# Turning the gated unit's output by VectorE blocks and on-chip transfers instead of by TensorE

## The chip, the cores and the metric

The kernel runs on one core of a Trainium2 chip. The metric is the device time of one execution in microseconds (us). A profile of one execution shows what each engine did: PE is TensorE (PEld its weight loads), DVE is VectorE, ACT is ScalarE, POOL is GpSimd, SP is the engine that issues most transfers (SPq in rows). Each engine takes its instructions strictly in the order in which the program lists them.

## The reference, cut to what matters

Two layers, each with one mixer over 256 tokens of width 2048. All columns come from one input projection. The change touches the gated unit of the convolution branch: `u` is made token by token, and the convolution runs along the tokens, channel by channel.

```python
proj = jnp.einsum("bsd,de->bse", h, w_in[layer])
q, k, v, g_att, glu_a, glu_b, g_conv = jnp.split(proj, SPLIT_POINTS, axis=-1)
...
u = glu_a * jax.nn.sigmoid(glu_b)
u = jnp.pad(u, ((0, 0), (CONV_WIDTH - 1, 0), (0, 0)))
y = lax.conv_general_dilated(u, dw_kernel.astype(u.dtype)[:, None, :], window_strides=(1,),
                             padding="VALID", dimension_numbers=("NWC", "WIO", "NWC"),
                             feature_group_count=D_CONV) + dw_bias
y = jax.nn.silu(layer_norm(y, ln_g, ln_b))
return jnp.einsum("bsc,ce->bse", y, w_pw)
```

## The kernel before, in words

All matrix products are cut into groups of 512 output columns, 40 for each layer, and each group into 8 tiles: 640 tiles in one fixed order, numbered 0 to 639 here. A tile is 256 rows of weights, 512 KB. Four things happen to tile i. SP issues its load into one of four buffers `raw` (`load`, line 222). ACT copies it to the rounded half `whi` (line 229). DVE forms the rest `wlo` by a subtraction (line 230). PE runs 12 matmuls on it (lines 616 to 618), the second of which is the first to need `wlo`. The load of tile i stands on SP right behind the split of tile i-4, whose buffer it takes, and `whi` and `wlo` have four buffers each, so a split of tile i can start when PE has finished tile i-4.

All other work is written as generators, and a planner (`Filler`) with its own clock for each engine places their slices between the tiles when the program is built. So the order on every engine is fixed; a slice that comes late on the chip holds what is listed behind it.

For each block j of 512 channels (four in a layer) the groups are glu_b, glu_a, v, q, k. `ev_glu_b` leaves the sigmoid in `Dt[0]`, 128 partitions (tokens) by 2 token halves by 512 channels. `ev_glu_a` multiplies it in place by glu_a on DVE (line 314). Then PE turns the result by 8 transposes through the identity into two PSUM banks (`transposes`, line 256), and ACT copies the banks to `uT` (line 322), which has channels on partitions. The convolution (`conv`, lines 336 and 339) reads `uT` on DVE, 124 operations for each j. In the first layer and j = 1, which the rows below follow, glu_a is tiles 48 to 55 and the transposes stand on PE between tiles 56 and 57.

Of the kernel before, what the change touches and what calls it, by code (L numbers as in the profile page):

```python
# [13 lines left out]
AF = mybir.ActivationFunctionType  # L14
# [3 lines left out]
SEQ = 256  # L18
# [3 lines left out]
PAD = CW - 1  # L22
KT = D // 128
NCH = 4
CH = 512
# [14 lines left out]
class Need:  # L40
# [3 lines left out]
    def __init__(self, banks=0, when=None, **time):  # L44
        self.banks, self.when, self.time = banks, when, list(time.items())
# [5 lines left out]
class Filler:  # L51
# [7 lines left out]

    def __init__(self, banks, horizon, patience):  # L60
        self.tasks = []
        self.t = dict(P=0.0, V=0.0, A=0.0, G=0.0)
        self.horizon, self.patience = horizon, patience
        self.banks = [(b, 0.0) for b in banks]
        self.count = 0
# [80 lines left out]
def trunk(ctx: ExitStack, tc: tile.TileContext, x, w_in, q_norm_g, k_norm_g, w_pw, w_out, x_t, gains, params,  # L146
          rope_cos, rope_sin, log_count, out):
    nc = tc.nc
# [4 lines left out]
    V, S, G, T = nc.vector, nc.scalar, nc.gpsimd, nc.tensor  # L153

    def t(shape, name, dt=F32):
        return sb.tile(shape, dt, name=name)
# [5 lines left out]
    A = [t([128, 2, CH], f"a{c}") for c in range(4)]  # L162
# [3 lines left out]
    uT = [t([128, 4, PAD + SEQ], f"ut{i}") for i in range(2)]  # L166
# [3 lines left out]
    qT, kT = (C[i].rearrange("p (h s) -> p h s", h=4) for i in (1, 2))  # L170
    Dt = [t([128, 2, CH], f"d{i}") for i in range(3)]
    t2 = t([128, CH], "t2")
    sm = [t([128, 384], f"sm{i}") for i in range(4)]
    junk = t([128, CH], "junk", BF16)
    ident = t([128, 128], "ident")
# [21 lines left out]
    fill = Filler([pp.tile([128, CH], F32, name=f"ax{i}") for i in range(4)], dict(V=4.5, A=3.5), 5)  # L197
# [41 lines left out]
    def flag(*what):  # L239
        flags.add(what)  # L240

    def has(*what):
        return lambda: what in flags
# [6 lines left out]
    def transposes(src, banks):  # L250

        for b in range(2):
            for i in range(2):
                for tt in range(2):
                    e = (2 * b + i) * 128
                    T.transpose(banks[b][:, i * SEQ + tt * 128:i * SEQ + tt * 128 + 128],  # L256
                                src[:, tt, e:e + 128], ident)

    def to_stationary(src, s, c, gain):

        yield Need(2, lambda: vacant[s][c], P=0.9)
        banks = [fill.bank(), fill.bank()]
        transposes(src, banks)
        yield Need(A=1.5, V=1.6)
        p = [b[:, i * SEQ:(i + 1) * SEQ] for b in banks for i in range(2)]
        for i in range(4):
            S.activation(st_hi[s][c][:, i], p[i], AF.Copy, scale=gain(i))  # L267
        for i in range(4):
            V.scalar_tensor_tensor(st_lo[s][c][:, i], p[i], gain(i), st_hi[s][c][:, i].bitcast(F32),  # L269
                                   op0=ALU.mult, op1=ALU.subtract)  # L270
        fill.free(*banks)
        filled(s, c)

    def filled(s, c):
        vacant[s][c] = False
        ready[s][c] = True
# [12 lines left out]
    def x_chunk(l, c):  # L289

        yield from to_stationary(A[c], 0, c, lambda i: ng[:, l * KT + 4 * c + i:l * KT + 4 * c + i + 1])
        fill.add(x_square(l, c), 3, fill.now[4])
# [18 lines left out]
    def ev_glu_a(l, j, ps):  # L311
        yield Need(0, has("ev", l, "glu_b", j), V=1.4)
        for tt in range(2):
            V.scalar_tensor_tensor(Dt[0][:, tt], ps[tt], rx[:, tt:tt + 1], Dt[0][:, tt],
                                   op0=ALU.mult, op1=ALU.mult)
        flag("ev", l, "glu_a", j)
        yield Need(2, has("conv", l, j - 2) if j >= 2 else None, P=0.9)
        banks = [fill.bank(), fill.bank()]
        transposes(Dt[0], banks)
        yield Need(A=1.0)  # L320
        for b in range(2):
            S.activation(uT[j % 2][:, 2 * b:2 * b + 2, PAD:], banks[b].rearrange("p (c s) -> p c s", c=2), AF.Copy)
        fill.free(*banks)
        flag("glu", l, j)
        fill.add(conv(l, j), 5 + j, fill.now[4])

    def conv(l, j):
        u = uT[j % 2]
        y = Y[j].rearrange("p (c s) -> p c s", c=4)
        w = prm[:, 4 * j:4 * j + 4]  # L330
        for k in range(CW):
            for c in range(4):
                if c % 2 == 0:
                    yield Need(V=0.8)
                if k == 0:
                    V.tensor_scalar(y[:, c], u[:, c, 0:SEQ], w[:, c, l * CW:l * CW + 1], w[:, c, P_BIAS + l:P_BIAS + l + 1],
                                    op0=ALU.mult, op1=ALU.add)
                else:
                    V.scalar_tensor_tensor(y[:, c], u[:, c, k:k + SEQ], w[:, c, l * CW + k:l * CW + k + 1], y[:, c],  # L339
                                           op0=ALU.mult, op1=ALU.add)  # L340
        flag("conv", l, j)
        for c in range(4):
            yield Need(0, has("ysum", l, j - 1) if j else None, G=0.7)
            if j == 0 and c == 0:
                G.tensor_copy(ysum, y[:, c])
            else:
                G.tensor_add(ysum, ysum, y[:, c])  # L347
        flag("ysum", l, j)
        if j == NCH - 1:
            fill.add(layer_norm(l), 4, fill.now[4])  # L350
# [166 lines left out]
    def ev_g_att(l, j, ps):  # L517
        yield Need(0, has("attsq", l, j), A=1.2, V=1.2)
        for tt in range(2):
            S.activation(Dt[0][:, tt], ps[tt], AF.Silu, scale=rx[:, tt:tt + 1])  # L520
        V.tensor_mul(A[j], A[j], Dt[0])
        flag("ev", l, "g_att", j)
        yield from to_stationary(A[j], 0, j, lambda i: prm[:, 4 * j + i, P_ATT + l:P_ATT + l + 1])
        src = x[0, :, j * CH:(j + 1) * CH] if l == 0 else xs[j]
        nc.sync.dma_start(A[j], src.rearrange("(t p) e -> p t e", p=128))
# [7 lines left out]
    def ev_pw(l, j, ps):  # L533
        yield Need(A=1.2, V=1.2)
        y = Y[j].rearrange("p (t e) -> p t e", t=2)
        for tt in range(2):
            V.tensor_mul(y[:, tt], ps[tt], GC[j][:, tt])
            S.activation(junk, ps[tt], AF.Square, accum_out=ssf[:, tt, j:j + 1])
        flag("ev", l, "pw", j)
        if j == NCH - 1:  # L540
            yield Need(V=0.1, G=0.6)
            V.tensor_reduce(rsc, ssf, axis=mybir.AxisListType.X, op=ALU.add)
            rsqrt(rc, rsc, 1.0 / D, 2)
            flag("rc", l)
        yield from to_stationary(y, 1, j, lambda i: prm[:, 4 * j + i, P_CONV + l:P_CONV + l + 1])
# [44 lines left out]
    for c in range(NCH):  # L590
        fill.add(first_chunk(c), 0)
    split(0)


    users = {"glu_b": ev_glu_b, "glu_a": ev_glu_a, "v": ev_v, "g_conv": ev_g_conv, "g_att": ev_g_att,
             "pw": ev_pw, "o_att": ev_o_att, "o_conv": ev_o_conv,
             "q": lambda l, j, ps: ev_qk(l, j, ps, "q"), "k": lambda l, j, ps: ev_qk(l, j, ps, "k")}
    last = {0: ("g_conv", "o_att"), 1: ("pw", "o_conv")}
    for i, (g, s) in enumerate(tiles):
        l, nm, j, _, _, _, st = groups[g]  # L600
        c = s * KS // 4
# [18 lines left out]
        if later and (i == 0 or i % 2):  # L620
            dst, src, c = later.pop(0)
# [65 lines left out]
```

## Time and profile before

| What | us |
|---|---|
| median of 3 runs (1860.91 to 1862.95) | 1862.9 |
| the profiled execution, device time | 1864.4 |
| its span (first to last instruction) | 1862.6 |
| PE busy | 1848.9 |
| DVE busy | 1392.2 |
| ACT busy | 989.0 |

The profiled execution took 1.8 us more than its span and 1.5 us more than the median. Busy time of PE is that of matmuls whose ends are modelled and overlap, so the pace of PE is read from starts: in a steady stretch one matmul starts every 0.227 us and one tile every 2.72 us.

### The profile page before, as it was taken

What the parts mean: (1) busy time and instruction counts of PE and PEld (TensorE: products, weight loads), DVE (VectorE), ACT (ScalarE), POOL (GpSimd) and SP (SyncE); (2) the same over time, 40 slices, a digit from 0 to 9 for tenths busy, and PEclk for the clock granted to TensorE, in tenths of its full rate; (3) what the DMA queues carried; (4) which work ended last, traced back from release to release, by engine and by line L of the source; (5) the groups of instructions that cost most, each with busy time, mean ns of one, the idle gap of its engine ahead of it and who ended that gap; (6) DMA issues with size and microseconds to landing.
All of it is one profiled execution on the core that took longest, in us unless ns stands there. A gap on an engine that the chain in (4) does not pass through costs nothing.

```text
span 1862.6 us, 23725 instructions
## 1 busy us (share of the span) xinstructions
PE 1848.9 (99%) x8490; PEld 1536.0 (82%) x8490; DVE 1392.2 (75%) x2157; ACT 989.0 (53%) x1559; POOL 139.8 (8%) x153
## 2 busy tenths in 40 slices
PE   8999999999999999999999999999999999999999
PEld 5788888888888888888888888888888888888887
DVE  5678889788889876556558888797887998755554
ACT  5565564554654456445444655646556445644542
POOL 2010100100110141000000101002000102100000
PEclk9999999999999999999999999999999999999999
DMA  8665656656566676556666656565565666666564
GB/s 268 218 184 168 180 179 180 183 167 190 175 179 193 190 225 203 193 189 191 208 203 192 186 162 184 160 197 183 162 183 167 193 194 190 213 204 194 180 204 147
DMA packets 181527, 352.06 MB, mean 189 GB/s; under 512 B 11248, under 2 KB 11248, under 8 KB 181408
## 3 DMA queue, kind: packets, MB, share of 16 engines
q1 hardware_dynamic: 179584, 347.19, 61.3%
q0 software_dynamic: 960, 1.77, 0.6%
q8 instruction: 66, 1.08, 0.2%
q10 hardware_dynamic: 864, 1.59, 0.2%
q14 instruction: 53, 0.43, 0.1%
HBM read 346.31 MB, written 4.19 MB: 188 GB/s over the span
## 4 chain that ended last, share of the span: by engine, by line
PE 97%; DMA 2%; ACT 0%; issue 0%; DVE 0%; SPq 0%; POOL 0%; ACTq 0%; DVEq 0%
PE acc L616 31%; PE acc L618 31%; PE acc L617 31%; PE ax L256 2%; DMA a<-in_x 1%; DMA raw<-in_w_in 1%; PE ax L465 1%; PE ax L482 1%; PE ax L490 0%; PE ax L491 0%; PE ax L489 0%; PE ax L464 0%; DMA y<-in_x_t 0%; ACT whi L229 0%; DVE wlo L230 0%
## 5 line engine op out<-in xcount | busy, mean ns | idle before, releaser
L230 DVE TENSOR_TENSOR wlo<-raw,whi 128x1024 fp32r<-128x1024 f32 x640 | 792.6, 1247 | 413.5 <-ACT whi L229 407.4
L229 ACT ACTIVATE whi<-raw 128x1024 fp32r<-128x1024 f32 x640 | 675.3, 1063 | 657.7 <-PE acc L618 466.3
L616 PE MATMUL acc<-whi,sthi 128*128 128x512 f32 x2560 | 1005.5, 393 | 6.0 <-ACT sthi L283 5.4
L617 PE MATMUL acc<-wlo,sthi 128*128 128x512 f32 x2560 | 997.8, 390 | 2.3 <-DVE wlo L230 2.3
L618 PE MATMUL acc<-whi,stlo 128*128 128x512 f32 x2560 | 998.2, 390 | 0.0
L616 PEld LDWEIGHTS acc<-whi,sthi 128*128 128x128 f32 x2560 | 481.6, 188 | 105.6 <-ACT sthi L283 6.3
L618 PEld LDWEIGHTS acc<-whi,stlo 128*128 128x128 f32 x2560 | 481.2, 188 | 101.5 <-DVE stlo L285 1.0
L617 PEld LDWEIGHTS acc<-wlo,sthi 128*128 128x128 f32 x2560 | 481.6, 188 | 100.9 <-DVE wlo L230 3.2
L339 DVE SCALAR_TENSOR_TENSOR y<-ut,prm,y 128x256 f32<-128x256 f32 x960 | 408.6, 483 | 0.0
L427 POOL TENSOR_SCALAR qr<-qss 128x8 f32<-128x8 f32 x16 | 3.2, 198 | 696.8 <-ACT junk L424 696.8
L347 POOL TENSOR_TENSOR ysum<-ysum,y 128x256 f32<-128x256 f32 x30 | 36.5, 1218 | 240.8 <-DVE y L339 133.5
L424 ACT ACTIVATE junk<-acc,rx 128x128 bf16<-128x128 f32 x128 | 47.1, 368 | 8.4 <-PE acc L618 4.8
L434 ACT ACTIVATE d<-acc,qr 128x128 f32<-128x128 f32 x128 | 34.8, 383 | 15.8 <-POOL qr L429 15.8
L267 ACT ACTIVATE sthi<-ax,prm 128x256 fp32r<-128x256 f32 x64 | 25.1, 476 | 30.7 <-PE ax L256 30.7
L269 DVE SCALAR_TENSOR_TENSOR stlo<-ax,prm,sthi 128x256 fp32r<-128x256 f32 x64 | 26.5, 475 | 14.4 <-ACT sthi L267 14.4
L455 ACT ACTIVATE c<-ax 128x512 f32<-128x512 f32 x32 | 17.4, 596 | 33.6 <-PE ax L256 33.6
L478 ACT ACTIVATE sm<-sm,smm 128x128 f32<-128x128 f32 x64 | 28.2, 443 | 6.6 <-DVE smm L473 6.6
L375 POOL TENSOR_TENSOR ssum<-ssum,d 128x512 f32<-128x512 f32 x14 | 28.5, 2033 | 6.5 <-ACT d L368 5.6
L428 POOL TENSOR_TENSOR qr<-qr,half 128x8 f32<-128x8 f32 x16 | 26.3, 1642 | 1.3
L256 PEld LDWEIGHTS ax<-ident,d 128*128 128x128 f32 x192 | 22.4, 140 | 3.2
L256 PE MATMUL ax<-ident,d 128*128 128x128 f32 x192 | 24.9, 273 | 0.0
L424 ACT ACTIVATION_READ_ACCUMULATOR junk<-acc,rx 128x1 f32 x128 | 24.7, 193 | 0.0
(105 smaller groups left out, 659.3 us busy)
## 6 DMA issues: line engine op xcount, KB each, us to landing
raw<-in_w_in SPq DMA_DIRECT2D x448, 512.0 KB, 4.1
raw<-in_w_out SPq DMA_DIRECT2D x128, 512.0 KB, 4.7
raw<-in_w_pw SPq DMA_DIRECT2D x64, 512.0 KB, 4.6
a<-in_x SPq DMA_DIRECT2D x8, 512.0 KB, 6.0
xs<-a SPq DMA_DIRECT2D x4, 512.0 KB, 6.5
a<-xs SPq DMA_DIRECT2D x4, 512.0 KB, 6.6
y<-in_x_t SPq DMA_DIRECT2D x3, 512.0 KB, 12.4
out<-a SPq DMA_DIRECT2D x4, 256.0 KB, 6.0
```

The lines of the kernel that those rows point to most:

```text
L229: S.activation(hi, a, AF.Copy)
L230: V.tensor_sub(wlo[i % R_SPLIT], a, hi.bitcast(F32))
L256: T.transpose(banks[b][:, i * SEQ + tt * 128:i * SEQ + tt * 128 + 128], src[:, tt, e:e + 128], ident)
L339: V.scalar_tensor_tensor(y[:, c], u[:, c, k:k + SEQ], w[:, c, l * CW + k:l * CW + k + 1], y[:, c], op0=ALU.mult, op1=ALU.add)
L347: G.tensor_add(ysum, ysum, y[:, c])
L375: G.tensor_add(ssum, ssum, half_sq)
L424: S.activation(junk[:, :DH], ps[tt][:, h * DH:(h + 1) * DH], AF.Square, scale=rx[:, tt:tt + 1], accum_out=qss[:, tt, h:h + 1])
L434: S.activation(n[:, tt, h * DH:(h + 1) * DH], ps[tt][:, h * DH:(h + 1) * DH], AF.Copy, scale=qr[:, tt, h:h + 1])
L478: S.activation(s[:, cs], s[:, cs], AF.Exp, bias=m[:, tt:tt + 1], scale=-1.0, accum_out=lsum[:, tt:tt + 1])
L616: T.matmul(ps[tt], xh, hi[:, kk], start=(k == 0), stop=False)
L617: T.matmul(ps[tt], xh, lo[:, kk], start=False, stop=False)
L618: T.matmul(ps[tt], xl, hi[:, kk], start=False, stop=(k == KT - 1))
```

## The change

The 8 transposes on PE and the two copies out of PSUM go. Instead DVE turns each 32 by 32 square in place with two instructions (one for each token half) into a new tile `blocks`, 16 transfers on SP's queue carry 32 by 256 pieces of `blocks` back into `Dt[0]` under other partitions, and ACT copies the result to `uT` with four instructions. The planner gets a clock Q, on which the 16 transfers count as 5 us. The descriptor space of transfers issued by POOL is cut to 4096 bytes a partition, which makes room for `blocks`.

```diff
+    blocks = t([128, 2 * CH], "blocks")
...
+    def turn(z):
+        yield Need(V=1.3)
+        for tt in range(2):
+            V.transpose(blocks.rearrange("p (b c t j) -> p t c b j", b=4, c=4, t=2)[:, tt],
+                        z[:, tt].rearrange("p (c b j) -> p c b j", c=4, b=4))
+        yield Need(Q=5.0)
+        flat = z.rearrange("p t e -> p (t e)")
+        for a in range(4):
+            for b in range(4):
+                nc.sync.dma_start(flat[32 * b:32 * b + 32, a * SEQ:(a + 1) * SEQ],
+                                  blocks[32 * a:32 * a + 32, b * SEQ:(b + 1) * SEQ])
...
         flag("ev", l, "glu_a", j)
-        yield Need(2, has("conv", l, j - 2) if j >= 2 else None, P=0.9)
-        banks = [fill.bank(), fill.bank()]
-        transposes(Dt[0], banks)
-        yield Need(A=1.0)
-        for b in range(2):
-            S.activation(uT[j % 2][:, 2 * b:2 * b + 2, PAD:], banks[b].rearrange("p (c s) -> p c s", c=2), AF.Copy)
-        fill.free(*banks)
+        yield from turn(Dt[0])
+        yield Need(0, has("conv", l, j - 2) if j >= 2 else None, A=1.6)
+        turned = Dt[0].rearrange("p t e -> p (t e)").rearrange("p (a c t j) -> p c t a j", a=4, c=4, t=2)
+        for c in range(4):
+            S.activation(uT[j % 2][:, c, PAD:].rearrange("p (t a j) -> p t a j", t=2, a=4), turned[:, c], AF.Copy)
         flag("glu", l, j)
...
-    nc = bacc.Bacc("TRN2", target_bir_lowering=False, num_devices=1)
+    nc = bacc.Bacc("TRN2", target_bir_lowering=False, num_devices=1, dynamic_dma_scratch_size=4096)
```

On SP, in the first layer and j = 1, the change now lists the transfers behind the load of tile 64 (the first row; before, only loads stood here). DMAHW0 to DMAHW7 are the eight completion semaphores that SP's transfers take in turn, and a transfer waits for the last one that used its semaphore.

```order
L223 DMA raw0_89<-in_w_in 128x2x512 [waits DMAHW6_49,DVE_49]
L272 DMA d0_107<-blocks_111 32x256 x4
L272 DMA d0_107<-blocks_111 32x256 [waits DMAHW7_49]
L272 DMA d0_107<-blocks_111 32x256 [waits DMAHW0_49]
L272 DMA d0_107<-blocks_111 32x256 [waits DMAHW1_49]
L272 DMA d0_107<-blocks_111 32x256 [waits DMAHW2_49]
L272 DMA d0_107<-blocks_111 32x256 [waits DMAHW3_49]
```

The load in the first row itself uses DMAHW2, so the eighth transfer waits until that load has landed; the ninth (last row) to the sixteenth wait for the first to the eighth, and the loads of tiles 65, 66 and 67 stand behind all of them.

On ACT before, the two copies from PSUM stood between the copies `whi` of tiles 59 (first row) and 60:

```order
L229 ACTIVATE whi3_96<-raw3_92 128x1024 [waits DMAHW5_49,DVE_49,PE_49]
L322 ACTIVATE ut1_102<-ax2_159 128x2x256 [waits PE_49]
L322 ACTIVATE ut1_102<-ax3_160 128x2x256 [waits PE_49]
L229 ACTIVATE whi0_93<-raw0_89 128x1024 [waits DMAHW6_49,DVE_49]
L229 ACTIVATE whi1_94<-raw1_90 128x1024 [waits DMAHW7_49,DVE_49,PE_49]
```

With the change, the four copies stand between `whi` of tiles 62 (second row) and 63 (fifth row):

```order
L230 ACTIVATE whi1_94<-raw1_90 128x1024 [waits DMAHW7_49,DVE_49,PE_49]
L230 ACTIVATE whi2_95<-raw2_91 128x1024 [waits DMAHW0_49,DVE_49,PE_49]
L337 ACTIVATE ut1_102<-d0_107 128x256 [waits DMAHW4_49,DMAHW3_49,DMAHW5_49,DMAHW2_49,DMAHW6_49,DMAHW1_49,DMAHW7_49,DMAHW0_49,DVE_49]
L337 ACTIVATE ut1_102<-d0_107 128x256 x3
L230 ACTIVATE whi3_96<-raw3_92 128x1024 [waits DVE_49,PE_49]
```

They moved three tiles later, and the first of them waits for all eight semaphores, that is for all 16 transfers, with `whi` of tile 63 behind it. The other seven turns (tiles 24, 104, 144, 344, 384, 424 and 464 on SP) are listed in the same way.

## Rows read from the trace of the kernel before

**Rows 1.** The page's part 1: busy us, share of the span, instructions.

```profile
PE 1848.9 (99%) x8490; PEld 1536.0 (82%) x8490; DVE 1392.2 (75%) x2157; ACT 989.0 (53%) x1559; POOL 139.8 (8%) x153
```

**Rows 2.** Waits of PE: who waited, for whom, us in total, times, longest.

```profile
PE acc L616 <- ACT sthi L283: 5.4, 2, 3.2
PE acc L617 <- DVE wlo L230: 2.3, 3, 0.8
```

**Rows 3.** Timeline of PE from 182 us: start us, us, engine, line, operation, count.

```profile
182.39 0.39 PE L616 MATMUL acc<-whi,sthi 128*128 128x512 f32 x1
...
184.88 0.40 PE L618 MATMUL acc<-whi,stlo 128*128 128x512 f32 x1
185.12 1.04 PE L256 MATMUL ax<-ident,d 128*128 128x128 f32 x8
...
186.46 0.39 PE L618 MATMUL acc<-whi,stlo 128*128 128x512 f32 x1
```

**Rows 4.** Timeline of PE from 65.5 us, the first layer's j = 0.

```profile
66.64 0.40 PE L618 MATMUL acc<-whi,stlo 128*128 128x512 f32 x1
66.88 1.04 PE L256 MATMUL ax<-ident,d 128*128 128x128 f32 x8
...
68.22 0.39 PE L618 MATMUL acc<-whi,stlo 128*128 128x512 f32 x1
```

**Rows 5.** The instructions of line 322: duration in ns, first and last start.

```profile
L322 ACT ACTIVATE ut<-ax x16: 592/598/598, 67.5 to 1343.5; 128x512 f32<-128x512 f32 x16
```

**Rows 6.** Timeline of DVE from 180 us.

```profile
181.08 1.22 DVE L230 TENSOR_TENSOR wlo<-raw,whi 128x1024 fp32r<-128x1024 f32 x1
182.21 1.40 DVE L314 SCALAR_TENSOR_TENSOR d<-acc,rx,d 128x512 f32<-128x512 f32 x2
...
195.47 1.22 DVE L230 TENSOR_TENSOR wlo<-raw,whi 128x1024 fp32r<-128x1024 f32 x1
```

**Rows 7.** Timeline of PE from 200.5 us: where tile 63 begins.

```profile
202.33 0.39 PE L616 MATMUL acc<-whi,sthi 128*128 128x512 f32 x1
```

**Rows 8.** Timeline of ACT from 178 us, in brackets its idle time and what ended it.

```profile
185.75 1.09 ACT L322 ACTIVATE ut<-ax 128x512 f32<-128x512 f32 x2 [2.11 <-PE ax L256]
186.73 1.06 ACT L229 ACTIVATE whi<-raw 128x1024 fp32r<-128x1024 f32 x1
```

**Rows 9.** Timeline of SP's queue at the start: issues back to back.

```profile
0.73 0.94 SPq L222 DMA_DIRECT2D raw<-in_w_in  x2
1.72 0.46 SPq L567 DMA_DIRECT2D y<-in_x_t  x1
```

**Rows 10.** Issues from 58 to 63 us: count, size, median us to landing.

```profile
raw<-in_w_in SPq DMA_DIRECT2D x4, 512.0 KB, 5.0
```

**Rows 11.** The same from 186 to 195 us.

```profile
raw<-in_w_in SPq DMA_DIRECT2D x3, 512.0 KB, 3.9
```

**Rows 12.** From 1859 us to the end: transfer engines' busy tenths (0.09 us slices), an issue.

```profile
DMA  5999999620000005999999620000000000000000
...
out<-a ACTq DMA_DIRECT2D x1, 256.0 KB, 2.1
```

**Rows 13.** Timeline of ACT from 8.3 us: four copies of 128x256 in SBUF.

```profile
8.44 1.71 ACT L283 ACTIVATE sthi<-y,ng 128x256 fp32r<-128x256 f32 x4 [2.50 <-DMA y<-in_x_t]
10.06 1.04 ACT L229 ACTIVATE whi<-raw 128x1024 fp32r<-128x1024 f32 x1
```

**Rows 14.** Timeline of DVE from 61 us, the first layer's j = 0.

```profile
63.98 1.23 DVE L230 TENSOR_TENSOR wlo<-raw,whi 128x1024 fp32r<-128x1024 f32 x1 [1.81 <-ACT whi L229]
65.12 1.41 DVE L314 SCALAR_TENSOR_TENSOR d<-acc,rx,d 128x512 f32<-128x512 f32 x2
```

**Rows 15.** Timeline of ACT from 30 us: it waits for a transfer.

```profile
50.41 0.63 ACT L297 ACTIVATE junk<-a 128x512 bf16<-128x512 f32 x1 [4.93 <-DMA a<-in_x]
```

**Rows 16.** Timeline of PE from 51.5 us.

```profile
54.15 0.50 PE L617 MATMUL acc<-wlo,sthi 128*128 128x512 f32 x1 [0.76 <-DVE wlo L230]
```

**Rows 17.** Timeline of POOL from 0 us: its last wait before `rx`.

```profile
54.27 0.18 POOL L247 TENSOR_SCALAR rx<-rsc 128x2 f32<-128x2 f32 x1 [16.56 <-DVE rsc L301]
```

More of the change, by code (lines that the diff above doesn't have):

```diff
@@ L61, in __init__ @@
         self.tasks = []
-        self.t = dict(P=0.0, V=0.0, A=0.0, G=0.0)
+        self.t = dict(P=0.0, V=0.0, A=0.0, G=0.0, Q=0.0)
         self.horizon, self.patience = horizon, patience
```

## The prediction, made before the changed kernel ran

> **What bounds the kernel now.** I read the page's busy times first: PE works for 99% of the span [rows 1]. Then the waits of PE, to see whether it ever stands: 5.4 us for the first inputs and 2.3 us for `wlo`, and nothing else of weight [rows 2]. So the time is the sum of what PE has to start, and an instruction taken off PE shortens the span one for one, as long as PE still finds its operands ready. How early they are ready is the second thing to read. Tile 63 begins on PE at 202.33 us [rows 7]. Its `wlo` was begun at 195.47 and took 1.22 us [rows 6], so it lay ready for 5.6 us. That is the cushion on which the change leans: ACT and DVE run their splits about two tiles ahead.
>
> The trace also holds an instance of the cushion running out. At 50.41 us ACT had stood 4.93 us for a transfer, with copies `whi` queued behind it [rows 15], and PE then waited 0.76 us for a `wlo` [rows 16]. An ACT instruction that waits for transfers is what the change adds.
>
> **What it removes.** From the last matmul ahead of the transposes to the third behind them is 184.88 to 186.46, 1.58 us [rows 3]; three matmuls at the steady pace (a tile of 12 runs from 182.39 to 185.12) take 0.68. So a turn costs PE 0.90 us, the block and the slower first matmuls behind it. The first turn of the kernel shows the same 1.58 [rows 4]. Line 322 has 16 copies, two for each turn [rows 5], so there are eight turns, and 8 x 0.90 = **7.2 us** leave PE. The two copies on ACT go too, which hid behind its idle time [rows 8].
>
> **What it adds, followed in j = 1 of the first layer.** I keep the clock of the old trace and leave the block out: PE then starts tile 57 at 185.12 [rows 3], and tile 63, six tiles of 2.72 later, at 201.4; `wlo` of tile 63 is wanted by the second matmul, at **201.66**.
>
> DVE: the split of tile 58 at 181.08 and the two products are unmoved; the products end at 183.61 [rows 6]. The two block transposes are new to the trace. The nearest rows are these products: 512 elements a partition, 0.70 us each. A floor is half the pace of the subtraction, which moves 1024 elements from 181.08 to 182.21: 0.57. A ceiling is two passes at its duration, 1.22 for 512 elements. Nothing in the rows suggests two passes, so I take 0.62 each, 1.25 together: they end at 184.95 (0.1 us lies ahead of them). They push the split of tile 59 to 186.17, and that of tile 60, whose `whi` ACT can now make from 185.3 to 186.4, to 187.63. The other DVE work is hidden by the cushion.
>
> SP: the load of tile 64 goes out at 187.66, 1.5 us behind that of tile 63. Loads 1.1 us apart landed after 5.0 us [rows 10], loads further apart after 3.9 [rows 11]; I take 4.5, so 192.15. Issues without a wait follow each other every 0.5 us (two loads and the next issue: 0.73 to 1.72 [rows 9]); for these small pieces the trace shows nothing cheaper, and 0.4 is my lower bound. The eighth transfer would go at 191.6, but its semaphore is the load's, so it goes at 192.2. Eight more steps of 0.5: the sixteenth goes at 196.2. How long does a 32 KB transfer take to land? The nearest row is a 256 KB store at the end with nothing beside it: 2.1 us, of which the engines are busy for some 8 slices of 0.09, about 0.7 [rows 12]. So 1.4 is the floor, 2.1 the ceiling; a small piece lies near the floor, and I take 1.45. Everything has landed at **197.65**.
>
> Here a rule of the Trainium skill speaks against the change: "DMA: Bandwidth & Descriptors", section "Rules for kernel authors", says that many small transfers should be coalesced, since under 64 KB one pays mostly overhead; the page's fit elsewhere is about 2.0 us fixed for each transfer (for transfers issued by GpSimd). With it the last piece would land at 198.3 and the sum below would come to about 1862.3. The row's 1.4 us besides data agrees on the kind of cost, at a smaller size.
>
> ACT: it has made `whi` of tile 62 and stands from about 192 until 197.75. Four copies of 128x256 take 1.62 us until the next instruction starts (8.44 to 10.06 [rows 13]). So `whi` of tile 63 runs 199.4 to 200.4 and `wlo` to **201.67**, against 201.66 wanted. The cushion of 5.6 us is used up to the last tenth, and PE stands for about nothing. Behind it, DVE has four convolution steps before `wlo` of tile 64, as long as PE's tile, and lighter tiles after; the lag does not grow. The load of tile 65 goes out at 196.7, lands near 201, and ACT comes to it at 202.5: hidden. The first later turn finds the cushion restored, since 40 tiles lie between turns.
>
> The first turn of the first layer is worse. There the split of tile 18 ran at 63.98 to 65.2, 1.81 us held up by its `whi` [rows 14], so the products end at 66.53, transposes at 67.85, splits of tiles 19 and 20 at 69.05 and 70.2. The load goes at 70.2 with another 1.15 us ahead of it: landed at 75.2. Eighth transfer 75.25, sixteenth 79.25, landed 80.7, copies until 82.4. DVE has the first convolution steps ahead of this `wlo`, which therefore ends at 84.9. PE wants it at 66.88 [rows 4] + 16.32 + 0.23 = 83.4. PE stands **1.5 us**.
>
> The last edit, less descriptor space for POOL, I cost at nothing: POOL stands 16.56 us before it makes `rx` [rows 17], which covers slower table loads. The convolution begins about three tiles later, which moves the layer norm; by the program's order it is still done some 13 tiles, 35 us, ahead of its first user.
>
> **The sum.** -7.2, +1.5 for the first turn, +0.5 for seven turns at the edge: -5.2. The profiled 1864.4 becomes 1859.2, its span 1857.4. That execution was 1.5 us above the median of the runs, so I state **1857.7**. Each 0.1 us by which the chain of a turn is longer than I have it costs 0.8 us over eight turns; 0.9 us of standing in every turn eats the gain.
>
> **The rivals.**
> - The transfers are quicker: issues every 0.4 us and landings of 3.9 and 1.4 make the chain 1.4 us shorter, and nothing waits but 0.1 in the first turn: 1855.8. For it: the pieces are small. Chance 0.20.
> - The last landing takes 2.1 us, as the 256 KB row does whole: the chain is 0.65 longer, seven turns wait 0.66, the first 2.15: 6.8 us, 1862.5, no change. By the skill's rule above it is this case that comes. For it: most of that row is not data. Chance, with all chains 0.25 to 1.2 us too long, 0.27.
> - On the other side: the block transposes take 1.22 us each, for strided squares are not plain streams. Each chain is 1.2 us later: 7 x 1.2 + 2.7 = 11.1 us, 1866.8, slower. The gain is gone from 0.98 us a transpose on (8 x 0.71 + 1.5 = 7.2), and from about 1.2 it would be measured as slower. Against it: every 512-element row of DVE here is near 0.7. Chance of this or another chain over 1.2 us too long: 0.15.
> - The forecast, within some 0.25 us of the computed chain: 0.38.
>
> **How the numbers follow.** A measurement of this kernel tells 0.2%, 3.7 us, from no change. Faster (under 1859.2) are the forecast and the quick transfers, 0.58; no change 0.27; slower 0.15. The range goes from 1854.5, no wait at all and a quick set of runs, to 1865, a chain 1 us too long: what lies above has some 0.17. The likeliest case's own range is 1856 to 1859.
>
> **What would show it.** The 64 transposes are gone and matmuls run on through each turn. ACT waits 4 to 6 us for a transfer into `d` ahead of the first `uT` copy. The eighth transfer goes out just when the load ahead of it lands. DVE's transposes are near 0.7 us long. PE's waits for `wlo` grow by less than 3 us, most of it near 83 us. The prediction is wrong if PE waits for `wlo` in every turn, if issues are dearer than 0.5 us, or if a landing takes 2 us or more.

## The result, and the profile after

The changed kernel takes **1877.2 us** (median of 4 runs, 1875.91 to 1877.28); the kernel before, run beside it, 1862.9. The ratio is 1.0073, with a 95% interval of 1.006 to 1.0086. It was forecast at 1857.7 with a range up to 1865: wrong in sign and outside the range. The profiled span is 1874.1 us, against 1862.6 before. Two executions stand far outside all others, one of the kernel before (10746 us) and one of the version with half of the transfers on POOL (2656 us, at a granted clock of 0.65), and count in no ratio below.

The page's busy times [rows 1] and the first two lines of its chain that ended last:

```profile
PE 1846.2 (99%) x8426; PEld 1529.0 (82%) x8426; DVE 1402.1 (75%) x2173; ACT 989.3 (53%) x1575; POOL 140.7 (8%) x153
...
PE 89%; DMA 5%; SPq 2%; ACT 2%; DVE 1%; issue 1%; ACTq 0%; POOL 0%; DVEq 0%
PE acc L631 28%; PE acc L632 28%; PE acc L630 28%; DMA raw<-in_w_in 3%; SPq L272 2%; PE ax L257 2%; ACT whi L230 1%; DVE wlo L231 1%; DMA d<-blocks 1%; PE ax L479 1%; DMA a<-in_x 1%; PE ax L496 1%; ACT ut L337 0%; PE ax L503 0%; PE ax L505 
```

PE is as busy as before by share, and has 64 instructions less. A busy share of 99% hides what happened, since 1% of this span is 19 us. The chain tells it: it leaves PE for the transfers' issues (line 272), their landings, ACT and the loads. The waits of PE, beside those of before [rows 2]:

```profile
PE acc L630 <- ACT whi L230: 8.0, 9, 1.4
PE acc L631 <- DVE wlo L231: 7.3, 9, 1.0
PE acc L630 <- ACT sthi L299: 7.1, 2, 3.8
```

The last row is the start of the kernel. The first two are new in size and come nine times each, eight of them in the turns. Behind them stands ACT; the group of the four copies, busy time and mean on the left, idle time ahead of them on the right:

```profile
L337 ACT ACTIVATE ut<-d 128x256 f32<-128x256 f32 x32 | 10.7, 406 | 67.0 <-DMA d<-blocks 67.0
```

ACT stands for the transfers 67.0 us in eight turns, 8.4 each, where 4 to 6 were forecast.

Now j = 1 of the first layer, engine by engine. DVE, against [rows 6]:

```profile
182.49 1.40 DVE L330 SCALAR_TENSOR_TENSOR d<-acc,rx,d 128x512 f32<-128x512 f32 x2
183.81 1.29 DVE L266 STREAM_TRANSPOSE blocks<-d 128x512 f32<-128x512 f32 x2
...
202.47 1.23 DVE L231 TENSOR_TENSOR wlo<-raw,whi 128x1024 fp32r<-128x1024 f32 x1 [7.55 <-ACT whi L230]
```

The block transposes cost nearly what was forecast, 1.29 us for both instead of 1.25. DVE then waits 7.55 us for the `whi` of tile 63. SP's queue, load 64 first, then the first, the eighth, the fifteenth and sixteenth transfer, and load 65:

```profile
187.92 0.37 SPq L223 DMA_DIRECT2D raw<-in_w_in  x1
188.34 0.52 SPq L272 DMA_DIRECT2D d<-blocks  x1
...
193.10 0.51 SPq L272 DMA_DIRECT2D d<-blocks  x1
...
197.45 1.23 SPq L272 DMA_DIRECT2D d<-blocks  x2
198.78 0.53 SPq L223 DMA_DIRECT2D raw<-in_w_in  x1
```

Issues of load 64 and of the sixteenth transfer alone, with the time to landing at the end of the row:

```profile
raw<-in_w_in SPq DMA_DIRECT2D x1, 512.0 KB, 5.2
...
d<-blocks SPq DMA_DIRECT2D x1, 32.0 KB, 1.8
```

The load lands at 187.92 + 5.2 = 193.1, and the eighth transfer goes at 193.10: the wait on its semaphore is there, as forecast. From the eighth to the end of the sixteenth is 193.10 to 198.68, nine issues, and two of them (a step and a duration of 0.59) take 1.23, so a step is near 0.63. ACT, in brackets its wait:

```profile
191.01 1.06 ACT L230 ACTIVATE whi<-raw 128x1024 fp32r<-128x1024 f32 x1 [1.66 <-DVE y L353]
200.15 1.34 ACT L337 ACTIVATE ut<-d 128x256 f32<-128x256 f32 x4 [8.07 <-DMA d<-blocks]
201.39 3.89 ACT L230 ACTIVATE whi<-raw 128x1024 fp32r<-128x1024 f32 x4
```

And PE, where tile 63 begins [rows 7]:

```profile
201.47 0.39 PE L632 MATMUL acc<-whi,stlo 128*128 128x512 f32 x1
202.49 0.50 PE L630 MATMUL acc<-whi,sthi 128*128 128x512 f32 x1 [0.63 <-ACT whi L230]
203.75 0.50 PE L631 MATMUL acc<-wlo,sthi 128*128 128x512 f32 x1 [0.76 <-DVE wlo L231]
204.08 0.39 PE L632 MATMUL acc<-whi,stlo 128*128 128x512 f32 x1
```

From the first to the last of these starts is 2.61 us, where three steady steps take 0.68: this turn loses 1.93 us. Comparing the starts of like-numbered tiles in the two traces, and giving each turn the 0.90 of the block removed, the eight turns lose 2.76, 1.94, 2.67, 4.23, 2.27, 1.9, 2.7 and 1.63, about 20 us. Between turns the two kernels run at one pace.

ACT stands before the copies of these turns for 8.65, 8.07, 8.75, 8.73, 8.15, 8.02, 8.83 and 7.75 us, together the 67.0. In seven turns the loss is this time less 5.9 to 6.1 us: that much of ACT's standing the cushion takes, and the rest comes out on PE. The fourth turn loses 1.6 us more than that; the part on why the prediction was wrong returns to it.

### The profile page after: what moved, and what is told of

Read it like the earlier page. It is cut to its first block, busy times and chain, and to the rows that moved or that the text cites. A ratio compares the mean times of both kernels' runs of the same rounds, so it can differ in the third digit from the quotient of the medians.

```text
span 1874.1 us, 23803 instructions
## 1 busy us (share of the span) xinstructions
PE 1846.2 (99%) x8426; PEld 1529.0 (82%) x8426; DVE 1402.1 (75%) x2173; ACT 989.3 (53%) x1575; POOL 140.7 (8%) x153
## 4 chain that ended last, share of the span: by engine, by line
PE 89%; DMA 5%; SPq 2%; ACT 2%; DVE 1%; issue 1%; ACTq 0%; POOL 0%; DVEq 0%
PE acc L631 28%; PE acc L632 28%; PE acc L630 28%; DMA raw<-in_w_in 3%; SPq L272 2%; PE ax L257 2%; ACT whi L230 1%; DVE wlo L231 1%; DMA d<-blocks 1%; PE ax L479 1%; DMA a<-in_x 1%; PE ax L496 1%; ACT ut L337 0%; PE ax L503 0%; PE ax L505 0%
## 5 line engine op out<-in xcount | busy, mean ns | idle before, releaser
L361 POOL TENSOR_TENSOR ysum<-ysum,y 128x256 f32<-128x256 f32 x30 | 31.0, 1035 | 268.5 <-DVE y L353 169.9
L337 ACT ACTIVATE ut<-d 128x256 f32<-128x256 f32 x32 | 10.7, 406 | 67.0 <-DMA d<-blocks 67.0
L350 DVE TENSOR_SCALAR y<-ut,prm 128x256 f32<-128x256 f32 x32 | 13.9, 482 | 15.2 <-ACT ut L337 15.2
```

## The experiments

Three theories of the 20 us stood against each other. A: ACT is held, in its fixed order, by the 16 transfers, with `whi` queued behind the copies. B: the weight loads that stand behind the transfers on SP land late. C: the block transposes fill DVE. Each diff is against the changed kernel.

**Copies later in ACT's order.**

```diff
-        yield Need(Q=5.0)
+        yield Need(Q=12.0)
```

> Edit: the planner counts the 16 transfers as 12 us instead of 5, so the four copies to uT stand two or three tiles later on ACT (behind whi of tiles 24, 65, 105 and so on); all instructions are kept and SP's order is the same. Three theories of the 20 us for which PE stands in the eight turns: A, ACT is held by the 16 transfers with whi queued behind its copies; B, the loads that stand behind the transfers on SP land late; C, the block transposes fill DVE. A: load 65 landed at 202.64 and its wlo is wanted near 207, so nothing stands: 1877.2 - 20 = 1857, from 1855 to 1859, faster than the kernel before. B and C: loads and transposes are where they were, so about 1877.

Measured: 1855.41 us (1853.35 to 1856.64), ratio to the kernel before 0.9961 (0.9948 to 0.9974). PE's waits are back at the level of before:

```profile
PE acc L630 <- ACT sthi L299: 4.7, 2, 2.4
PE acc L576 <- DVE junk L574: 1.4, 1, 1.4
PE acc L631 <- DVE wlo L231: 1.3, 2, 0.8
...
PE acc L630 <- ACT whi L230: 0.5, 1, 0.5
```

The timeline of ACT in j = 1:

```profile
193.48 1.06 ACT L230 ACTIVATE whi<-raw 128x1024 fp32r<-128x1024 f32 x1 [1.66 <-DVE y L353]
199.75 1.06 ACT L230 ACTIVATE whi<-raw 128x1024 fp32r<-128x1024 f32 x1 [5.21 <-DMA raw<-in_w_in]
200.72 1.32 ACT L337 ACTIVATE ut<-d 128x256 f32<-128x256 f32 x4
```

No copy waits here any more. ACT's wait has moved to the load of tile 65, which stood behind the transfers, so B's delay is real; but PE needs that tile later and does not feel it. In each of the eight turns PE now starts its tiles exactly 0.90 us earlier against the kernel before, so nothing is lost. A holds, B and C fall as causes of the loss. The median is the lowest of all versions, by less than their runs scatter.

**Copies that wait for no transfer.**

```diff
-        turned = Dt[0].rearrange("p t e -> p (t e)").rearrange(
+        turned = blocks.rearrange(
```

> Edit: the four copies read blocks and not the exchanged tile, so that they wait for no transfer; the 16 transfers are still issued on SP and the loads still stand behind them. The exchange is left out of the result. A: ACT is never held, the 20 us go: about 1857. B: the loads are as late as before, about 1877. C: the transposes are still there, about 1877.

Measured: 1855.69 us (1854.57 to 1857.18), ratio 0.9964 (0.995 to 0.9978). The copies' group, with nothing ahead of it:

```profile
L337 ACT ACTIVATE ut<-blocks 128x256 f32<-128x256 f32 x32 | 10.6, 402 | 0.0
```

The order on every engine is the changed kernel's; only the wait is gone, and with it 21.5 us.

**No transfers at all**: the same edit, and the loop of `dma_start` taken out together with its `Need(Q=5.0)`, so that the copies also stand earlier on ACT.

> Edit: as the kernel whose copies read blocks, and the 16 transfers of each turn are not issued either; block transposes and copies stay. The exchange is left out of the result. A and B: about 1857, and against the kernel that still issues the transfers A expects no difference within 1 us, B about 20 us. C: about 1877, since DVE has the same work.

Measured: 1856.41 us (1855.94 to 1857.14), ratio 0.9968 (0.9956 to 0.9979): 0.7 us from the kernel that still issues them. So the transfers cost PE nothing by themselves, and C falls again. These three versions keep the smaller descriptor space of POOL's transfers, so that edit is not the cause either. One row is used below, the load of tile 64 when no transfer stands behind it:

```profile
raw<-in_w_in SPq DMA_DIRECT2D x1, 512.0 KB, 4.4
```

**All transfers on POOL's queue.**

```diff
-                nc.sync.dma_start(flat[32 * b:32 * b + 32, a * SEQ:(a + 1) * SEQ],
+                G.dma_start(flat[32 * b:32 * b + 32, a * SEQ:(a + 1) * SEQ],
```

> Edit: the 16 transfers of a turn are issued by POOL and not by SP; the order of PE, DVE and ACT is the same, and SP has loads alone. On POOL two loads of gbc were issued in 1.08 us, 0.54 each, and landed after 4.1; the blocks are ready at 185.1 us in j = 1, so the last piece would be issued near 193.7 and land between 195.5 and 197.8, where on SP it landed at 199.9. A: the hold is 2.1 to 4.4 us shorter, so stalls of 1.6 to 2.8 us in seven turns vanish or nearly, that of 4.1 leaves up to 2: 1857 to 1861. B: loads are free, 1857. C: about 1877. If POOL's issues cost 1 us each, the last lands near 203 and A expects 1895 or more, B still 1857.

Measured: 1859.44 us (1856.08 to 1860.7), ratio 0.9981 (0.9972 to 0.999). POOL's issues in j = 1, then ACT's `whi` of tile 62 and its copies:

```profile
182.74 4.99 POOL L272 DMA_DIRECT2D d<-blocks  x10 [47.75 <-DVE blocks L266]
...
191.88 0.50 POOL L272 DMA_DIRECT2D d<-blocks  x1 [0.50 <-DMA d<-blocks]
...
188.37 1.06 ACT L230 ACTIVATE whi<-raw 128x1024 fp32r<-128x1024 f32 x1 [1.66 <-DVE y L353]
196.34 1.34 ACT L337 ACTIVATE ut<-d 128x256 f32<-128x256 f32 x4 [6.91 <-DMA d<-blocks]
```

The chain begins when the blocks are ready, without waiting for load 64, and steps by 0.50. ACT is released 3.8 us earlier by the clock than in the changed kernel, but this kernel also reaches tile 62 2.6 us earlier (188.37 against 191.01), so the hold is only 1.2 us shorter, 6.91 us instead of 8.07; over the eight turns it is 51.0 us instead of 67.0, 2.0 each, just under the 2.1 to 4.4 that was worked out. A piece lands only after 4.1 us in the median. PE still waits 2.7 us for `wlo`, in five places, four of them in the turns, and the turns lose 3.4 us. The time lies in A's window. No load stands behind transfers here, so the losses that are left are not B's: where a turn still loses over 0.1 us, it loses the hold less 5.9 to 6.1 us, as in the changed kernel.

**Half of the bytes.**

```diff
-                nc.sync.dma_start(flat[32 * b:32 * b + 32, a * SEQ:(a + 1) * SEQ],
-                                  blocks[32 * a:32 * a + 32, b * SEQ:(b + 1) * SEQ])
+                nc.sync.dma_start(flat[32 * b:32 * b + 32, a * SEQ:a * SEQ + 128],
+                                  blocks[32 * a:32 * a + 32, b * SEQ:b * SEQ + 128])
```

> Edit: each of the 16 transfers of a turn carries 32 by 128 elements, half of its bytes; count, queue and order are as in the changed kernel. Half of the exchange is left out of the result. If a transfer on this queue costs a fixed time of issue and landing whatever it carries, nothing changes: 1877, within 2 us, with steps near 0.63 and landings near 1.85. If bytes set step and landing, the chain from the eighth to the sixteenth is 2.5 us shorter by its steps and 0.9 by its landing, and of the stalls only about 0.6 us of the longest is left: 1856.

Measured: 1872.31 us (1871.65 to 1873.77), ratio 1.0053 (1.0038 to 1.0068). The transfers' own times don't move: durations in ns and first and last start, then ACT's wait for them in the eight turns, then least, median and most us to landing:

```profile
L272 SPq DMA_DIRECT2D d<-blocks x128: 507/589/1156, 70.3 to 1362.3; - x128
...
  ACT ut L337: 63.6, 8
...
DMA to landing us min/median/max: 1.7/1.8/5.2
```

Step and landing are fixed costs, as the first theory said; yet 4.9 us are saved, more than its 2. They came through the load ahead of the eighth transfer, which landed after 4.8 us instead of 5.2 in j = 1:

```profile
raw<-in_w_in SPq DMA_DIRECT2D x1, 512.0 KB, 4.8
```

There the hold is 0.4 us shorter; the eight holds are 63.6 us instead of 67.0, 3.4 less. The rest, some 1.6 us, is in the longest turn, which lost 1.55 instead of 4.23: its clock, told below, did not fall this time.

**Twelve transfers.**

```diff
-            for b in range(4):
+            for b in (b for b in range(4) if b != a):
```

> Edit: the four pieces of a turn that stay in their partitions are not sent, so that 12 transfers are left of 16. That part of the exchange is left out of the result. By the theory that the chain of 16 holds ACT, the hold is four steps of 0.635 us = 2.54 shorter, each turn's stall (2.76, 1.94, 2.67, 4.1, 2.27, 1.9, 2.7, 1.63, sum 20.0) falls by as much and not below nothing, and 2.1 us stay: 1855.4 + 2.1 = 1857.5. With steps of 0.5, as forecast, 4.5 would stay: 1859.9. If only the first seven landings or the load ahead of the eighth set the hold, and not the count behind it, 1877 stays.

Measured: 1856.29 us (1854.23 to 1857.08), ratio 0.9965 (0.9952 to 0.9977). ACT's copies in j = 1:

```profile
195.29 1.34 ACT L337 ACTIVATE ut<-d 128x256 f32<-128x256 f32 x4 [5.48 <-DMA d<-blocks]
```

The hold is 2.6 us shorter, where four steps of 0.63 are 2.5; so the count behind the eighth sets it. The estimate left 2.1 us of loss; in this trace the turns lose 0.2, mostly because the fourth turn's clock did not fall here either. The 0.9 us by which the median lies above that of the later copies are within the scatter of the runs.

**Copies one tile later, and one tile earlier.** The same line with `Q=8.0` and with `Q=3.0`.

> Edit: the planner counts the transfers as 8 us instead of 5, so the four copies stand one tile later on ACT (behind whi of tile 23, 63, 103 and so on). If the cushion is the distance of the copies from the tile that waits for ACT, each turn gains one tile's pace, 2.72 us: all stalls vanish but 1.4 us of the turn with 4.1, so 1855.4 + 1.4 = 1856.8, from 1855 to 1859. If a move by one tile only shifts the stall (whi of the next tile is as late, since ACT works through its queue without a gap), about 1870 or more.

> Edit: the planner counts the transfers as 3 us instead of 5, so the copies stand one tile earlier on ACT (behind whi of tile 21, 61, 101 and so on); nothing else is added or taken. If the cushion is counted in tiles between the copies and PE, every turn loses one tile's pace more: 1877.2 + 8 x 2.72 = 1899, from 1894 to 1902. If the copies' place does not matter and the gain of the later places came from something else in the new order, 1877 stays.

Later: 1856.42 us (1854.84 to 1859.02), ratio 0.9968 (0.9956 to 0.9981), as worked out. Earlier: 1911.49 us (1909.56 to 1912.2), ratio 1.0256 (1.0242 to 1.027), 34.3 above the changed kernel where 21.8 were expected. The waits of PE in that kernel:

```profile
PE acc L630 <- ACT whi L230: 29.4, 9, 4.4
PE acc L631 <- DVE wlo L231: 7.2, 11, 0.8
```

The wait for `whi` grew from 8.0 to 29.4, by 21.4 us: the tile's pace, eight times, as expected. What was missing from the estimate is the clock. Stretches of 2 us around PE's standing in j = 1; the columns are length, busy time and instructions of PE, PEld, DVE, ACT and POOL, the granted clock, the transfers' share and GB/s:

```profile
206.00:208.00 2.00, 0.03 (x1) 0.04 (x1) 0.05 (x1) 2.00 (x6) 0.00 (x0) 1.00 0.68 237
208.00:210.00 2.00, 1.24 (x3) 0.83 (x4) 2.00 (x4) 2.00 (x3) 0.00 (x0) 0.74 0.00 0
210.00:212.00 2.00, 2.00 (x7) 1.52 (x6) 2.00 (x4) 0.76 (x1) 0.00 (x0) 0.50 0.76 208
212.00:214.00 2.00, 2.00 (x10) 1.63 (x9) 2.00 (x5) 0.51 (x1) 0.00 (x0) 0.91 0.58 130
```

PE had stood from 204.74 to 207.97, 3.23 us, and again for 0.76 us. Then the granted clock is 0.50, that is 1.2 GHz instead of 2.4, and the row has 7 matmuls where the next one, at 0.91, has 10. The rest of the excess is (36.3 - 21.4) / 8 = 1.9 us for each turn by the spans (1910.4 and 1874.1). In j = 1 the slow stretch accounts for 1.5 us: seven steps of PE behind the second wait take 3.15 us, from 209.23 to 212.38, where they take 1.69 in the changed kernel.

**Half of the transfers on POOL, alone and with the copies one tile later.**

```diff
-                nc.sync.dma_start(flat[32 * b:32 * b + 32, a * SEQ:(a + 1) * SEQ],
+                (nc.sync if a < 2 else G).dma_start(flat[32 * b:32 * b + 32, a * SEQ:(a + 1) * SEQ],
```

> Edit: of the 16 transfers of a turn, 8 are issued by SP and 8 by POOL; PE, DVE and ACT keep the changed kernel's order. SP's eighth still waits for the load ahead of it, which landed at 193.1, and lands near 195; POOL's eight go from 185 on every 0.5 us and land after 4.1, near 193. By the theory of the chain the hold ends near 195 instead of 199.9 and all stalls vanish but some tenths: 1855.4 to 1857. If it is the number of transfers under way at once that makes each land late, the hold stays near 199 and the time above 1870.

> Edit: both cures together, half of the transfers on POOL and the copies one tile later. If each cure alone took away all that the chain costs, nothing is left to gain and the time is that of either, 1855.4 to 1856.4, within 1 us. If some of the chain's cost is still hidden in those two, 1853 or less.

Alone: median 1855.66 us (four of five runs 1853.0 to 1857.06), ratio 0.996 (0.9946 to 0.9974). ACT's copies in j = 1:

```profile
194.34 1.34 ACT L337 ACTIVATE ut<-d 128x256 f32<-128x256 f32 x4 [3.75 <-DMA d<-blocks]
```

The hold is 3.75 us instead of 8.07, and fits into the cushion of about 6. With the later copies too: 1856.38 us (1855.39 to 1856.99), ratio 0.9962 (0.9949 to 0.9976). Nothing more is gained: each cure alone reaches the floor, and the other versions near 1855.4 to 1856.4 can't be told apart from one another.

## Why the prediction was wrong

The mechanism was right and its size was not. The chain of j = 1, step by step, with the forecast's times moved by 0.25 us (PE starts tile 57 at 185.37 in this trace, where the forecast had 185.12):

| Step | forecast, us | measured, us |
|---|---|---|
| block transposes end | 185.2 | 185.10 |
| load 64 issued | 187.91 | 187.92 |
| load 64 landed | 192.4 | 193.1 |
| eighth transfer issued | 192.45 | 193.10 |
| sixteenth issued | 196.45 | 198.1 |
| sixteenth landed | 197.9 | 199.9 |
| copies begin to `whi` of tile 63 | 1.62 long | 1.24 long |
| `whi` of tile 63 begins | 199.65 | 201.39 |
| `wlo` of tile 63 ends | 201.92 | 203.70 |
| PE wants it | 201.91 | 201.92 |

- **What leaves PE**, 7.2 us: right. The later copies are 6.9 us faster than the kernel before, and in that trace each turn moves PE's tiles 0.90 us earlier.
- **DVE** and the place of load 64: right, within 0.1 us.
- **The failing step is ACT's: "PE stands for about nothing".** The chain was 1.78 us longer than I had it, and the whole cushion had been spent, so all of it came out on PE. In the sum, "+0.5 for seven turns at the edge" measured 17.3 us, and "+1.5 for the first turn" 2.76. Three terms of the chain were too small. "I take 4.5" for the load: 5.2 in j = 1 with 16 transfers behind it, 4.8 with half their bytes, 4.4 with none; the transfers slow the very load whose landing releases the eighth of them, 0.7 us. Of these only 0.4 are the load's alone, since at 0.63 a step the eighth could not have gone before 192.7. "Eight more steps of 0.5": eight of 0.63, 1.0 us more, the largest of the three. "I take 1.45" for the landing: 1.8, 0.4 us more. The copies were 0.4 us shorter than feared.
- **The price of the error** stood in the prediction: 0.8 us for each 0.1. With 1.78 that is 14.2 us, or 1872. Of the 5 us that are left the other turns account for 3.9. The first lost 2.76, less than its forecast 1.5 and the 1.78 together; the third and the seventh lost 2.7, the fifth 2.27. The fourth lost 4.23: its two waits are 1.28 and 0.76 us, and behind them the clock fell here too, as these stretches of 3 us of the changed kernel show (columns as above):

```profile
440.00:443.00 3.00, 1.64 (x7) 0.78 (x5) 0.60 (x1) 2.92 (x6) 0.00 (x0) 1.00 0.89 293
443.00:446.00 3.00, 2.32 (x7) 1.88 (x8) 3.00 (x6) 2.83 (x4) 0.00 (x0) 0.77 0.45 123
446.00:449.00 3.00, 3.00 (x10) 2.35 (x10) 3.00 (x7) 1.13 (x3) 0.00 (x0) 0.67 0.74 236
```

- **The rivals.** "The last landing takes 2.1 us" was nearest in kind and a third of the length. The Trainium skill's rule beside it, that under 64 KB one pays mostly overhead ("DMA: Bandwidth & Descriptors", section "Rules for kernel authors"), is borne out by the halved pieces, which cost the same step of 0.63 and landing of 1.8. The slower rival named the block transposes as its mechanism and was wrong in that: they took 0.65 us each. It was given 0.15 with "another chain over 1.2 us too long", which is what happened. Of the signs of being wrong that the prediction named, PE's waits for `wlo` in every turn and issues over 0.5 us came; the landing stayed under 2.
- **Where I chose wrongly.** The 0.5 us of a step was a row of 512 KB loads at the kernel's start, and 0.4 stood as a lower bound with no upper one beside it. The landing's 1.45 was taken next to its floor of 1.4, with a ceiling of 2.1, and the load's 4.5 in the middle between 3.9 and 5.0, and a sum that leaves a cushion of nothing has no room for that.

The turns differ (1.63 to 2.76 without the fourth) by how long the transfers held ACT, 7.75 to 8.83 us. The fourth's hold of 8.73 us would give 2.6; the other 1.6 came with the clock. Why the clock fell there stays open: the third and the seventh turn had waits as long, 1.30 and 1.38 us with 0.76 behind each, and their granted clock stayed at 1.00.

## What to carry to other kernels

An instruction that waits for transfers blocks everything behind it on an engine with a fixed order; list it later by the part of the wait that the cushion does not cover. Here the wait was about 8 us against a cushion of about 6, and one tile of 2.72 us was enough. That one number, 5 to 8 or 12 in the planner, turned 0.7% slower into 0.4% faster, with no instruction changed. Price small transfers by their count (here 0.63 us to issue on SP, 1.8 to land, and the ninth waits for the first), and where a sum ends with a cushion of zero, charge its error bars to every place that repeats it.

## What the runs showed of the hardware that was not expected

- A 32-partition transfer between partitions takes a step of 0.63 us on SP's queue and 0.50 on POOL's, and lands after 1.8 us at either 32 or 16 KB when nothing is ahead of it on SP.
- Small transfers delay a 512 KB load issued just before them: 4.6, 4.8 and 5.2 us with none, with 16 of half size and with 16 of full size behind it (means of the loads ahead of the eight turns; they reach from 4.4 to 4.9, 4.5 to 5.2 and 4.7 to 5.8).
- After PE had stood for 3.23 us and again for 0.76 the granted clock fell from 2.4 to 1.2 GHz for a few microseconds, so a stall cost more than its own length. After 0.63 and 0.76 us in j = 1 of the changed kernel it did not fall. The length of the waits alone does not tell: it fell after 1.28 and 0.76 us in the fourth turn, and not after 1.30 and 0.76 in the third or 1.38 and 0.76 in the seventh.
